# A hybrid decoder step: the samples' recurrence on VectorE, another closing order, and weight remainders by accumulating transfers

## The chip, the cores and the metric

The kernel runs on one core of one Trainium2 chip. Its five engines each have an instruction stream of their own: TensorE (PE) for matmuls and transposes, VectorE (DVE), ScalarE (ACT), GpSimd (POOL) and SyncE (SP). In this kernel SP issues nearly all transfers between DRAM and the on-chip memory (SBUF), and POOL issues a few. Matmul results land in a second on-chip memory (PSUM), which vector and scalar instructions read. The metric is the device time of one execution in microseconds (us).

## What is computed

The reference is one inference step of a two-layer decoder with width 1024, for a prompt of 1024 tokens and for 8 samples of one token each, which share all weights. Everything is float32. In outline, for the prompt and for the samples alike:

```
h = x
# layer 0
hn  = rmsnorm(h, g[0])
q, f, i, gate, q_m = split(hn @ w_in_a, 5)          # 512 columns each, 4 heads of 128
F = lb + (1 - lb) * sigmoid(f);  k = 1 - F;  v = i;  q = silu(q)
for each token: S = F[:, None] * S + k[:, None] * v[None, :];  o = q @ S     # per head, S is 128x128
mix = concat(rmsnorm(o) * silu(gate), attention(q_m, mem_k[0], mem_v[0])) @ w_o[0]
h = h + rmsnorm(mix);  h = h + rmsnorm(swiglu(rmsnorm(h)))
sb_k, sb_v = split(rmsnorm(h) @ w_kv)
# layer 1: stick-breaking attention over sb_k, sb_v (samples: over a paged cache), and memory attention
h = h + rmsnorm(concat(stick_breaking, attention(q_m, mem_k[1], mem_v[1])) @ w_o[1])
h = h + rmsnorm(swiglu(rmsnorm(h)))
swiglu(h) = (silu(h @ w_gate) * (h @ w_up)) @ w_down     # 2816 hidden columns: 22 blocks of 128
```

The samples start from given states `state_hgrn` (8 samples x 4 heads x 128 x 128) and take one step of the recurrence; the new states are an output (`st_sample`). Outputs also are `y_prompt`, `y_sample`, the shared keys and values, and the memory keys and values.

## The kernel before

**Split numbers.** TensorE multiplies in a format of fewer bits (float32r). So each operand is split into a rounded part and a remainder, and a product is made of three matmuls: high x high, high x low, low x high. For weights this is `split_w` (L196): a transfer of up to 4 blocks of 128x128 into `raw` (pool `wraw`, 5 buffers), a cast on ScalarE into `ws[:, 0]` (L206), and a subtraction on VectorE into `ws[:, 1]` (L207). The tiles `ws` come from the pool `wspl` with 5 buffers. `proj` (L212) calls it for the 4 or 8 blocks of a product and then issues the matmuls (L220). For activations it is `split_to` (L226).

**Tokens.** The prompt is worked in two halves: g = 0 has 512 columns, and g = 1 has the other 512 plus the 8 samples, 520 in all, done as two matmuls of 260. Activations stand with features on the partitions.

**Stages.** The program is a list of generators that `weave` merges by weights, step by step, so that the instruction streams hold pieces of several stages side by side. The framework's scheduler then orders each engine's instructions by priority and its own estimate of times, assigns buffers and sets the waits. Each engine works its own list in order. The stages that the change touches are:

- `hgrn_prompt` (L1147), the prompt's recurrence in 7 levels of doubling blocks, m = 1 to 64. At each level 16 calls per pair of heads and halves (L1174) make the products of a later block's queries with an earlier block's keys, 128 x m per chunk, and `copy_predicated` (L1184) puts them by a mask in the attention matrix `atts`.
- `hgrn_sample` (L1088), the samples' single step, woven with the gates and with part 1 of layer 0's feed-forward of g = 0. It turns k and v (L1096, L1097) so that samples stand on partitions, spreads v over a block diagonal (L1113), and makes k times v on TensorE (L1122). VectorE multiplies the state with F (L1117) and adds the product (L1123). For q times state, q is spread over a selection (L1105) and 32 small products go to TensorE (L1125). States come and go by SP (L1110, L1128).
- `ffn` (L697), the feed-forward of one half in five parts of 5, 5, 4, 4, 4 hidden blocks (`PARTS`). Each block has a gate and an up product over 8 blocks, and each part ends with 8 down products over its hidden blocks (L727). In layer 1 it serves g = 0 alone, beside the attention of g = 1 and of the samples, whose cache pages POOL fetches by index (L977).
- `weight_sums` (L549), sums of gate and up weights that POOL makes by accumulating transfers from DRAM to DRAM (L566; plain copies L568), each behind a tiny copy (L563) as a mark. They serve a multiplication scheme with fewer products (`ffn_w`, `gate_up_w`, L511), among other places in the last stage, layer 1's feed-forward of g = 1.
- `close` (L664), the last down products of that stage, with TensorE holding tokens on the moving side. It runs once for columns 0 to 255 (a = 0) and once for columns 256 to 519 with the samples (a = 1); weights are split in the first pass and kept for the second. After each pass `out_rows.finish` (L762) turns the result to rows, scales, adds the residual (L782, L785) and stores (L790; the samples L792).

## Time and profile before

| what | value |
|---|---|
| median of 3 runs (lowest, highest) | 2471.2 us (2469.78, 2472.68) |
| the profiled execution | 2472.22 us |
| its span, first to last instruction | 2470.5 us |
| granted clock of TensorE, mean | 0.999 |
| busy: TensorE, VectorE, ScalarE, POOL | 99%, 66%, 50%, 7% of the span |
| moved by transfers | 395.29 MB |

The profile's page gives busy times, a map of the span in 40 slices, the chain of work that ended last, groups of instructions, and transfers. A row of a group has the line, engine and operation, the tiles written and read, the count, then busy us and mean ns of one, then the idle time of the engine just before them and who ended it. A row of the chain has its start, its length in us and the work. TensorE's records overlap in the pipeline, so what a matmul costs is read from the distance of starts, or from the chain, and not from its own duration.

### The profile page before, as it was taken

Reading aid. Unit: us, or ns where it says so; the run is one execution under the profiler, and the core shown is the slowest. Engines: PE = TensorE matmul, PEld = TensorE weight load, DVE = VectorE, ACT = ScalarE, POOL = GpSimd, SP = SyncE. Lnnn points to the kernel's source line nnn. Section 1 sums busy time; section 2 is a strip of 40 time slices with the busy share of each in tenths; the row PEclk is TensorE's granted clock in tenths of the full one; section 3 lists DMA queues with packets and bytes.
Section 4 is the critical chain, followed back from the end, with each engine's and each line's share of the span. In section 5 each row is a group of like instructions: output and inputs, shape, how many; then the busy total and the mean of one; then the engine's idle time right before and its main releaser. Section 6 shows DMA issues by size and latency. Waiting matters only on the chain.

```text
span 2470.5 us, 42287 instructions
## 1 busy us (share of the span) xinstructions
PE 2436.5 (99%) x15971; PEld 2176.6 (88%) x15971; DVE 1639.5 (66%) x2988; ACT 1236.6 (50%) x2377; POOL 184.2 (7%) x316
## 2 busy tenths in 40 slices
PE   8999999999999999999999999999999999999998
PEld 6888888877879998899999989877777888999998
DVE  5767556754788685655756685778688466755666
ACT  5437544243445554555444554555554445664445
POOL 1000101100000000111200101212000100000000
PEclk9999999999999999999999999999999999999999
DMA  6354666546745437767666649754253573465542
GB/s 188 116 167 111 156 192 160 127 134 164 212 150 154 140 120 227 201 163 183 162 196 174 193 128 274 228 150 146 91 177 117 138 199 120 139 187 145 152 143 74
DMA packets 530503, 395.29 MB, mean 160 GB/s; under 512 B 21237, under 2 KB 468802, under 8 KB 530298
## 3 DMA queue, kind: packets, MB, share of 16 engines
q1 hardware_dynamic: 501114, 312.88, 42.4%
q0 software_dynamic: 29184, 79.70, 14.0%
q8 instruction: 126, 2.06, 0.3%
q14 instruction: 79, 0.65, 0.1%
HBM read 362.69 MB, written 101.11 MB: 188 GB/s over the span
## 4 chain that ended last, share of the span: by engine, by line
PE 88%; DVE 5%; DMA 3%; issue 2%; ACT 2%; POOL 0%; SPq 0%; DVEq 0%; ACTq 0%; POOLq 0%
PE mm L220 47%; PE q L511 13%; PE q L648 9%; PE q L464 3%; PE s L1174 2%; PE mm L1042 2%; PE s L906 1%; DMA c<-in_cache_mem_v 1%; PE s L1370 1%; PE mm L824 1%; PE mm L851 1%; PE q L680 1%; PE s L875 1%; PE s L1336 1%; PE s L899 1%
## 5 line engine op out<-in xcount | busy, mean ns | idle before, releaser
L220 PE MATMUL mm<-x,ws 128*128 128x260 f32 (+1 forms) x6240 | 1119.5, 335 | 3.2 <-DVE r L657 1.7
L220 PEld LDWEIGHTS mm<-x,ws 128*128 128x128 f32 x6240 | 941.6, 188 | 127.3 <-issue 2.7
L206 ACT CAST ws<-w 128x512 fp32r<-128x512 f32 (+1 forms) x652 | 382.8, 588 | 548.9 <-PE mm L220 396.9
L207 DVE TENSOR_TENSOR ws<-w,ws 128x512 fp32r<-128x512 f32 (+1 forms) x652 | 419.2, 648 | 253.5 <-ACT ws L206 243.5
L220 PE MATMUL mm<-m,ws 128*128 128x512 f32 (+1 forms) x1344 | 280.3, 360 | 0.5 <-DVE r L400 0.5
L220 PEld LDWEIGHTS mm<-m,ws 128*128 128x128 f32 x1344 | 218.0, 188 | 37.2 <-issue 1.0
L648 PE MATMUL q<-m,ws 128*128 128x260 f32 (+1 forms) x1824 | 221.7, 282 | 0.0
L648 PEld LDWEIGHTS q<-m,ws 128*128 128x128 f32 x1824 | 218.9, 188 | 1.1 <-DVE t L534 0.3
L502 DVE TENSOR_TENSOR ws<-w,ws 128x512 fp32r<-128x512 f32 x181 | 123.9, 690 | 87.6 <-ACT ws L501 86.1
L501 ACT CAST ws<-w 128x512 fp32r<-128x512 f32 x181 | 111.8, 621 | 109.2 <-PE q L648 32.5
L511 PE MATMUL q<-x,ws 128*128 128x260 f32 (+1 forms) x1188 | 158.1, 282 | 0.0
L511 PEld LDWEIGHTS q<-x,ws 128*128 128x128 f32 x1188 | 148.6, 188 | 0.0
L511 PE MATMUL q<-y,ws 128*128 128x260 f32 x912 | 119.9, 283 | 0.4 <-ACT q L521 0.2
L511 PEld LDWEIGHTS q<-y,ws 128*128 128x128 f32 x912 | 113.7, 189 | 1.1 <-ACT q L518 0.6
L464 PE MATMUL q<-x,ws 128*128 128x260 f32 (+1 forms) x720 | 91.3, 284 | 0.3 <-DVE r L400 0.2
L464 PEld LDWEIGHTS q<-x,ws 128*128 128x128 f32 x720 | 88.4, 188 | 1.8 <-DVE r L400 0.5
L511 PE MATMUL q<-a,ws 128*128 128x260 f32 (+1 forms) x672 | 87.1, 282 | 0.0
L511 PEld LDWEIGHTS q<-a,ws 128*128 128x128 f32 x672 | 83.2, 188 | 0.0
L657 DVE TENSOR_TENSOR r<-r,q 128x260 f32<-128x260 f32 (+1 forms) x128 | 48.4, 420 | 48.8 <-PE q L648 48.8
L237 DVE TENSOR_SCALAR t<-mm 128x512 f32<-128x512 f32 (+1 forms) x58 | 40.1, 691 | 54.1 <-PE mm L220 53.8
L563 POOL COPY mk<-a 128x1 f32<-128x1 f32 x36 | 21.0, 583 | 645.6 <-ACT a L1226 393.9
L228 DVE TENSOR_TENSOR m<-t,m 128x512 fp32r<-128x512 f32 (+1 forms) x88 | 60.8, 691 | 9.5 <-ACT m L227 8.7
(358 smaller groups left out, 3038.2 us busy)
## 6 DMA issues: line engine op xcount, KB each, us to landing
w<-in_w_gu SPq DMA_DIRECT2D x297, 256.0 KB, 3.4
w<-in_w_down SPq DMA_DIRECT2D x160, 256.0 KB, 2.8
wsum<-in_w_gu POOLq DMA_DIRECT2D x72, 512.0 KB, 6.5
w<-wsum SPq DMA_DIRECT2D x104, 256.0 KB, 3.5
w<-in_w_in_a SPq DMA_DIRECT2D x80, 256.0 KB, 3.3
w<-in_w_o SPq DMA_DIRECT2D x64, 256.0 KB, 2.8
wsum<-in_w_gu POOLq DMA_DIRECT2D x24, 640.0 KB, 7.0
wsum<-wsum POOLq DMA_DIRECT2D x24, 512.0 KB, 5.8
```

Source lines behind the costliest of these rows:

```text
L206: nc.scalar.copy(ws[:, 0, :n, :], raw[:, :n, :])
L207: nc.vector.tensor_sub(ws[:, 1, :n, :], raw[:, :n, :], ws[:, 0, :n, :].bitcast(F32))
L220: nc.tensor.matmul(ps[:, a, : PW[g]], wt, xt[k][:, xi, o : o + PW[g]], start=(k == 0 and wi == 0), stop=(k == nk - 1 and wi == 2),)
L228: nc.vector.tensor_sub(dst[1], src, dst[0].bitcast(F32))
L464: ins = nc.tensor.matmul(pp[a][:, :h], wt, xt[k][:, xi, a * h : (a + 1) * h], start=(k == 0 and wi == 0), stop=(k == ND - 1 and wi == 2),)
L501: nc.scalar.copy(w[:, 0, :], src)
L502: nc.vector.tensor_sub(w[:, 1, :], src, w[:, 0, :].bitcast(F32))
L511: nc.tensor.matmul(ps[:, :h], w[:, wj, k * P : (k + 1) * P], x[:, xi, :], start=(first and k == 0 and wi == 0), stop=(k == 3 and wi == 2), ...
L648: nc.tensor.matmul(pp[a][:, :h], wt, mids[k][:, xi, a * h : (a + 1) * h], start=(k == 0 and wi == 0), stop=(k == nf - 1 and wi == 2),)
L657: nc.vector.tensor_add(d, d, pp[a][:, :h])
L1042: nc.tensor.matmul(pb[i][:, a, :], xt[k][:, xi, c * P : (c + 1) * P], ws[:, s, :], start=(k == 0 and wi == 0), stop=(k == ND - 1 and wi == 2),
L1174: nc.tensor.matmul(plv[:, hh, c, :], K_[:, hh, cs], rhs, start=True, stop=True)
```

## The change

1. **The samples' recurrence.** k is no longer turned, and v is written to DRAM and read back broadcast over all partitions. VectorE multiplies the state with F, the broadcast v with k, adds them, and multiplies with q. TensorE then only sums over partitions: each half of a head's product is split and summed by two matmuls into one row of `po`, chosen by `selr`. The rows go through DRAM once more to be put in order. The constant `bdm` goes.
2. **The top level of `hgrn_prompt`** loads only the 64 key columns that are used, and puts the result by a plain copy on ScalarE.
3. **The closing order** becomes a = 1, then a = 0.
4. **Remainders by transfer.** In `ffn` of layer 1, g = 0, for the up and down weights: ScalarE writes the negated high part into the place of the remainder, and POOL issues a transfer that reads the weights from DRAM again and adds them there.

```diff
-    def split_w(W, k0, nk, m0, alloc=None):
+    def split_w(W, k0, nk, m0, alloc=None, acc=False):
...
             nc.scalar.copy(ws[:, 0, :n, :], raw[:, :n, :])
-            nc.vector.tensor_sub(ws[:, 1, :n, :], raw[:, :n, :], ws[:, 0, :n, :].bitcast(F32))
+            if acc:
+                nc.scalar.activation(ws[:, 1, :n, :], ws[:, 0, :n, :].bitcast(F32), AF.Copy, scale=-1.0)
+                nc.gpsimd.dma_start(ws[:, 1, :n, :], src, accum_op=ALU.add)
+            else:
+                nc.vector.tensor_sub(ws[:, 1, :n, :], raw[:, :n, :], ws[:, 0, :n, :].bitcast(F32))
...
-            for a in range(2):
+            for a in (1, 0):
...
-                    if a == 0:
+                    if a:
                         ws.append(split_w(w_down[l], f0, nf, m * P, self.spl4))
...
+            self.by_dma = g == 0 and l == 1
...
-                pu = proj(g, w_gu[l], 0, ND, DFF + (f0 + j) * P, self.xt)
+                pu = proj(g, w_gu[l], 0, ND, DFF + (f0 + j) * P, self.xt, self.by_dma)
...
-                ps = proj(g, w_down[l], f0, nf, m * P, mids)
+                ps = proj(g, w_down[l], f0, nf, m * P, mids, self.by_dma)
...
     def hgrn_sample(Ft, Kt, Qt, vs):
...
+        vd = tc.dram_tile([NB, 512], F32, name=nm("vd"))
+        nc.sync.dma_start(vd, vT[:NB, :])
+        yield
...
+            nc.sync.dma_start(vbv, vd[:, h * P : (h + 1) * P].partition_broadcast(P))
+            nc.vector.tensor_mul(stv, stv, col(Ft))
+            nc.vector.tensor_mul(vbv, vbv, col(Kt))
+            nc.vector.tensor_add(st, st, vb)
+            nc.sync.dma_start(st_sample[0, :, h].rearrange("b k v -> k b v"), stv)
+            nc.vector.tensor_mul(vbv, stv, col(Qt))
             for a in range(2):
-                ps = S()
-                nc.tensor.matmul(ps, kT[:NB, h * P : (h + 1) * P], vb[:NB, a, :], start=True, stop=True)
-                nc.vector.tensor_add(st[:, a, :], st[:, a, :], ps)
-            for b in range(NB):
-                nc.tensor.matmul(
-                    po[:NB, h * P : (h + 1) * P], qd[:, b, :], stv[:, b, :], start=(b == 0), stop=(b == NB - 1)
-                )
+                qs = B(F32R), B(F32R)
+                split_to(qs, vb[:, a, :])
+                for i, p in enumerate(qs):
+                    nc.tensor.matmul(
+                        po[:NB, :], selr[:, 2 * h + a, :], p,
+                        start=(h == 0 and a == 0 and i == 0), stop=(h == H - 1 and a == 1 and i == 1),
+                    )
+        rows = B()
+        nc.vector.tensor_copy(rows[:NB, :], po[:NB, :])
+        od = tc.dram_tile([H, NB, P], F32, name=nm("od"))
+        nc.sync.dma_start(od.rearrange("h (a b) v -> (h a) b v", a=2), rows[:NB, :].rearrange("p (b v) -> p b v", v=P))
         ot = B()
-        nc.vector.tensor_copy(ot[:NB, :], po[:NB, :])
+        nc.sync.dma_start(ot[:NB, :].rearrange("p (h v) -> p h v", v=P), od.rearrange("h b v -> b h v"))
...
+                        k = m if nbg == CH else P
+                        nc.tensor.matmul(
+                            plv[:k, hh, c, :], K_[:, hh, c * P : c * P + k], rhs, start=True, stop=True
+                        )
...
+                    if nb == 1:
+                        nc.scalar.copy(
+                            atts[hp * 2 + hh].rearrange("p (c t m) -> p c t m", c=CH, t=2)[:m, :, 1, :],
+                            plv[:m, hh, :, :],
+                        )
+                        continue
```

More of the change, by code (lines that the diff above doesn't have):

```diff
@@ L1088, in hgrn_sample, with col @@
     def hgrn_sample(Ft, Kt, Qt, vs):
-        HB = H * NB
-        kc = small([P, HB], tag="ss")
-        for h in range(H):
-            nc.vector.tensor_copy(kc[:, h * NB : (h + 1) * NB], Kt[h // 2][:, h % 2, G : G + NB])
-        pk = S()
         pvv = S()
         for h in range(H):
-            nc.tensor.transpose(pk[:NB, h * P : (h + 1) * P], kc[:, h * NB : (h + 1) * NB], ident)
             nc.tensor.transpose(pvv[:NB, h * P : (h + 1) * P], vs[:, h, :], ident)
-        kT = B()
-        nc.vector.tensor_copy(kT[:NB, :512], pk[:NB, :])
         vT = B()
         nc.vector.tensor_copy(vT[:NB, :512], pvv[:NB, :])
+        vd = tc.dram_tile([NB, 512], F32, name=nm("vd"))
+        nc.sync.dma_start(vd, vT[:NB, :])
+        yield
+        HB = H * NB
+        assert 2 * H == NB
         po = S()
         for h in range(H):
-            qd = small([P, NB, NB], tag="qd", bufs=2)
-            nc.vector.tensor_mul(
-                qd, sel, Qt[h // 2][:, h % 2, G : G + NB].unsqueeze(2).to_broadcast([P, NB, NB])
-            )
+            def col(t):
+                return t[h // 2][:, h % 2, G : G + NB].unsqueeze(2).to_broadcast([P, NB, P])
             st = C()
@@ L1173, in hgrn_prompt @@
                         rhs = Q_[:, hh, cs].rearrange("p (b t m) -> p b t m", t=2, m=m)[:, :, 1, :]
-                        nc.tensor.matmul(plv[:, hh, c, :], K_[:, hh, cs], rhs, start=True, stop=True)
+                        k = m if nbg == CH else P
+                        nc.tensor.matmul(
+                            plv[:k, hh, c, :], K_[:, hh, c * P : c * P + k], rhs, start=True, stop=True
+                        )
                 for hh in range(2):
@@ L1517, in tile_decoder @@
         nc.gpsimd.tensor_tensor(pidx, pidx, iot, op=ALU.add)
-        bdm = const.tile([NB, NB, 1], F32, name="bdm")
-        nc.gpsimd.affine_select(
-            bdm.rearrange("p b o -> p (b o)"), ones[:NB, :NB], pattern=[[-1, NB]], compare_op=ALU.is_equal,
-            fill=0.0, base=0, channel_multiplier=1,
-        )
     drain(head)
```

18 lines of the change are left out of this document (4 added, 14 removed).

## The prediction

> **What bounds the kernel now.** I read the page first (busy shares, chain by engine), then the chain of work and the waits of TensorE in the stages that the change touches, then single groups.
>
> ```profile
> span 2470.5 us, 42287 instructions
> PE 2436.5 (99%) x15971; PEld 2176.6 (88%) x15971; DVE 1639.5 (66%) x2988; ACT 1236.6 (50%) x2377; POOL 184.2 (7%) x316
> PE 88%; DVE 5%; DMA 3%; issue 2%; ACT 2%; POOL 0%; SPq 0%; DVEq 0%; ACTq 0%; POOLq 0%
> 520.00:616.00 96.00, 95.98 (x482) 73.22 (x481) 52.70 (x81) 36.26 (x61) 5.66 (x10) 0.98 0.56 152
> 1560.00:1955.00 395.00, 387.93 (x1887) 303.98 (x1886) 299.29 (x468) 207.46 (x399) 31.71 (x31) 1.00 0.47 140
> 1990.00:2092.00 102.00, 101.96 (x488) 83.94 (x487) 69.26 (x111) 52.35 (x85) 1.46 (x2) 1.00 0.52 152
> ```
>
> TensorE is busy all the time, and 88% of the chain is its work. The three window rows (length, then busy PE, weight loads, DVE, ACT, POOL; granted clock, DMA share) are the samples' recurrence, and the first half of layer 1's feed-forward in its two pieces. VectorE is at 76% in the second (299.29 of 395.00), and still TensorE is at 98%. So matmuls taken away are worth their own time; relief of VectorE is worth only what TensorE waits for it.
>
> **The samples' recurrence.** The chain from 520 to 620 us, by line, is in per cent of 100 us, so in us:
>
> ```profile
> by line: PE mm L220 80.2%; PE s L1125 8.4%; PE s L1122 7.6%; PE s L1213 0.9%; PE s L1209 0.9%; PE s L256 0.8%; PE s L1096 0.4%; PE s L1097 0.4%; PE s L1134 0.3%; PE s L1201 0.1%; issue 0.0%
> 1893.00 0.51 PE ns L948 x2
> 1918.04 0.46 PE ns L948 x2
> ```
>
> Gone are L1122 (k times v), L1125 (q times state) and L1096 (turning k): 7.6 + 8.4 + 0.4 = 16.4 us of TensorE. Added are 4 heads x 2 halves x 2 parts = 16 matmuls of the form of L948 (8 columns of `selr`, 512 moving): at 0.46/2 = 0.23 us, 3.7 us. Net 12.7 us less.
>
> ```profile
> L1117 DVE TENSOR_TENSOR c<-c,a x4: 1206/1214/1226, 354.5 to 561.7; 128x1024 f32<-128x1024 f32 x4
> L1113 DVE TENSOR_TENSOR c<-b,bdm x4: 1205/1210/1215, 528.8 to 564.1; 8x1024 f32<-8x1024 f32 x4
> L1105 DVE TENSOR_TENSOR qd<-sel,a x4: 224/224/226, 272.1 to 559.6; 128x64 f32<-128x64 f32 x4
> L1123 DVE TENSOR_TENSOR c<-c,s 128x512 f32<-128x512 f32 x8 | 5.4, 680 | 0.2 <-PE s L1122 0.2
> c<-in_state_hgrn SPq DMA_DIRECT2D x4, 512.0 KB, 5.4
> out_st_sample<-c SPq DMA_DIRECT2D x4, 512.0 KB, 4.9
> SPq L201 <- DVE ws L207: 1174.9, 506, 13.2
> ```
>
> VectorE per head: before 1.21 + 1.21 + 0.22 + 2 x 0.68 = 4.0 us; after 4 x 1.21 + 2 x 0.68 (split) = 6.2 us; four heads 9 us more, in a stage with 43 us idle: covered; without that cover it costs those 9 us. ScalarE gets 8 casts (5 us), also covered. SP gets 7 more transfers: v out to DRAM, four broadcasts of 512 KB back (5.4 us each by the state loads), and the rows out and back at the end. They stand in SP's queue ahead of weight loads, and a broadcast waits for the v write. SP is far ahead of need: 506 of its weight loads waited for a buffer that VectorE was still reading. I cost them at nothing; unhidden, each of the two round trips would cost about 10 us (5.4 + 4.9), bound 0 to 20. POOL loses one small select.
>
> **The top level of the prompt's scan (m = 64).** Its matmuls load 64 columns of K instead of 128, and eight predicated copies on VectorE become copies on ScalarE.
>
> ```profile
> 89.17 1.73 PE s L1174 x16
> L1174 PEld LDWEIGHTS s<-a,a x448: 186/192/193, 88.9 to 489.1; 128*128 128x128 f32 x150
> L1125 PEld LDWEIGHTS s<-c,qd x64: 85/90/133, 532.6 to 606.7; 128*8 128x8 f32 x64
> L1184 DVE COPY_PREDICATED b<-mask,s 128x256 f32<-128x256 uint8 x56 | 25.8, 525 | 0.0
> ```
>
> A record takes 1.73/16 = 0.108 us, though only 64 columns move, so I take the weight load to set its pace. A load of 128 columns takes 192 ns, of 8 columns 90: by a line between them, 64 columns take 138. The level has 448/7 = 64 records; 64 x 0.054 = 3.5 us is the upper end, 0 the lower; I take 2.0, since the next matmul can hide part. VectorE loses 8 x 0.525 = 4.2 us on which nothing waits, and ScalarE, idle half of the span, gains eight copies.
>
> The Trainium skill (TensorE: Matmul & The Clock Gate, LDWEIGHTS) says that a weight load's time is proportional to its columns alone, which would halve 0.108 and give 3.5 us. The trace disagrees at the small end, where 8 columns take 90 of 192 ns and not a sixteenth.
>
> **The closing order.** The chain's end, start and us:
>
> ```profile
> 2462.26 0.45 ACT yT L758
> 2465.87 0.65 DVE yT L782
> 2466.52 0.66 DVE yT L785
> 2467.21 0.30 SPq L792 DMA_DIRECT2D out_y_sample<-yT  x1
> DMA to landing us min/median/max: 2.6/2.6/2.6
> ```
>
> These rows are the sample's rows, which go to the middle, under the other half's matmuls. They free 0.45 + 0.65 + 0.66 = 1.8 us. But then the last store is a 512 KB row block, issued at about 2465.4 (2465.87 less 0.45) and landing 2.6 us later (the last row, that of the store of `y_prompt`), instead of the small one. I take 1.4 of the 1.8; lower end 0.5.
>
> **The remainders by DMA.** In layer 1's first half 22 x 2 up tiles and 56 down tiles (40 of 128x512, 16 of 128x128) are concerned: 100 subtractions leave VectorE, 100 negated copies go to ScalarE, and 100 accumulating transfers go to POOL's queue.
>
> ```profile
> L207 DVE TENSOR_TENSOR ws<-w,ws 128x512 fp32r<-128x512 f32 x588 | 401.4, 687 | 216.7 <-ACT ws L206 206.9 <-DMA w<-in_w_down 5.7 <-PE s L447 1.2
> L207 DVE TENSOR_TENSOR ws<-w,ws 128x128 fp32r<-128x128 f32 x64 | 18.3, 286 | 36.7 <-ACT ws L206 36.6
> L239 ACT ACTIVATE t<-t x42: 631/633/640, 399.4 to 1951.7; 128x512 f32<-128x512 f32 x32, 128x520 f32<-128x520 f32 x10
> L206 ACT CAST ws<-w 128x512 fp32r<-128x512 f32 x588 | 364.0, 620 | 473.6 <-PE mm L220 347.9 <-PE q L648 32.5 <-issue 24.7
> 1933.14 11.08 PE mm L220 x48
> wsum<-in_w_gu POOLq DMA_DIRECT2D x72, 512.0 KB, 6.5
> L566 POOL DMA_DIRECT2D wsum<-in_w_gu x64: 863/892/1297, 234.9 to 2000.0; - x64
> w<-in_w_gu SPq DMA_DIRECT2D x297, 256.0 KB, 3.4
> PE s L1370 <- ACT b L1367: 2.5, 2, 2.0
> 2000.02 0.87 POOL L566 DMA_DIRECT2D wsum<-in_w_gu  x1 [5.82 <-DMA wsum<-wsum]
> 2001.60 3.42 PE L220 MATMUL mm<-m,ws 128*128 128x512 f32 x14
> 1601.13 1.05 POOL L977 DMA_INDIRECT c<-in_cache_sb_k,pidx  x1 [26.04 <-DVE sc L934]
> PE s L1336 <- DVE b L1351: 1.1, 2, 0.8
> ```
>
> VectorE loses 84 x 0.687 + 16 x 0.286 = 62 us; ScalarE gains about 84 x 0.633 + 16 x 0.3 = 58 us, rising from 53% to about two thirds. The gain is bounded by TensorE's waits for vector work there; the rows of L1370 and L1336 are the longest of either kind, 3.6 us together. I take 2.0 less, bounds 0 and 4.
>
> The cost hangs on when a remainder is ready. A cast starts when TensorE frees one of five tiles (the release in L206's row). Four tiles lie ahead, 48 matmuls: 11.1 us, more where attention lies between. Down tiles of parts of five blocks have fewer, two tiles for 15 matmuls, so about 30: 7 us, but these parts are woven with attention. Against it stand the cast, 0.62, the negated copy, 0.63, and issue to landing. The nearest rows are a plain load of the same tile, 3.4, and a transfer of twice the size to DRAM, 6.5 (L566's accumulations hold POOL 0.89). Taking 4.5, nearer the plain load because bytes and shape are the same, the remainder is ready 5.8 us after the tile is free, at worst by these rows 7.8. So most of it is covered.
>
> Two places in POOL's queue are not. The sums for the last stage are still being made there; their last issue is at 2000.02, and the first down product of part 3 starts at 2001.60. An accumulation behind it lands at 2000.9 + 4.5 = 2005.4, its first use is two matmuls after 2001.60, at 2002.1: 3.3 us late, 5.3 by the 6.5; I take 4, bounds 0 and 6. And page loads of the cache hold POOL until VectorE frees a buffer (26.04 us once); accumulations behind one wait with it, and page loads now stand behind accumulations. Each was released by work of the same program place, so I take 2 for all of this, bounds 0 and 20.
>
> **The sum**, against the profiled execution's 2472.2 us: -12.7 - 2.0 - 1.4 - 2.0 + 4 + 2 = -12.1, so 2460.1. The median of the runs, 2471.2, is 1.0 lower: 2459.
>
> **Rivals.**
> *The remainders come too late (slower).* If a remainder needs N us from the freed tile, a turn of five tiles takes N plus a tile's own 2.8 us, or 13.9 when nothing waits. It decides from N = 11.1. With 100 tiles in some 20 turns, each us above costs about 20; N = 12.3 costs 24 and gives 2459 + 24 = 2483. For it: POOL's queue is in order, and ScalarE stands in the path twice. Against it: my estimate of 5.8, and 7.8 with the slower row.
>
> The Trainium skill (SBUF — State Buffer, A bandwidth-pool intuition that's wrong) bears on this rival. It says that descriptors of POOL's transfers cannot be written while VectorE runs a copy with both ports, and gives 3.1 us instead of 0.62. By that N would be some 2.5 us longer, 8.3, still under 11.1. The trace shows at most 1.30 against a usual 0.89 on L566.
>
> *The recurrence's matmuls go, but their time does not.* The new vector chain per head hangs on two loads, and at the end on two DRAM round trips. If TensorE stands in order before the 16 sums, 3 us per head eat 12 us: 2471, the same. Against it: 43 us of idle VectorE there.
>
> *All is hidden.* No collision at 2000 us, no late tile, both upper gains: -12.7 - 3.5 - 1.8 - 4 = -22, so 2449.
>
> **Chances.** Forecast 0.52, all hidden 0.17, recurrence without gain 0.13, too late 0.18. A difference under 0.2% (5 us) is no change to this measurement. Faster 0.69, same 0.13, slower 0.18. Range: from 2447, a little under all hidden, to 2483, the late case as priced; the forecast's own is 2452 to 2466.
>
> **What would show it.** Right: the chain from 520 to 620 has no L1122 or L1125, and 16 short products at 0.23 us; the sample's rows end before the last products; the new transfers land in 4 to 5 us; waits of TensorE for tiles whose remainder comes by DMA total under 10 us, most of it at the first down product of part 3. Wrong: landing over 9 us, or waits spread over all parts; or new waits of TensorE for the recurrence.

## The result, and the profile after

| | median (lowest, highest), us | ratio to before, 95% interval |
|---|---|---|
| before, beside it on the same chip | 2471.94 (2469.78, 2473.18) | |
| the changed kernel | 2492.85 (2488.54, 2496.17) | 1.0085 [1.0067, 1.0102] |

The change made the kernel 21 us slower. The prediction was 2459 us, and its range ended at 2483. The profiled execution took 2488.54 us; it is the lowest of its four runs, and 16.3 us above the profiled execution of before. The readings below explain these 16.3 us of the 21; the other runs have no profile.

The page of the changed kernel, by busy time, queues, chain, and groups:

```profile
span 2486.8 us, 42315 instructions
PE 2429.1 (98%) x15903; PEld 2174.4 (87%) x15903; DVE 1589.9 (64%) x2879; ACT 1291.2 (52%) x2493; POOL 311.3 (13%) x415
q1 hardware_dynamic: 505346, 315.02, 42.7%
q0 software_dynamic: 75840, 102.78, 21.5%
PE 83%; DMA 6%; DVE 5%; ACT 2%; issue 2%; POOL 0%; SPq 0%; DVEq 0%; ACTq 0%; POOLq 0%
L207 POOL DMA_DIRECT2D ws<-in_w_gu x44 | 57.9, 1352 | 180.1 <-ACT ws L206 146.9
L207 POOL DMA_DIRECT2D ws<-in_w_down x56 | 67.6, 1264 | 90.8 <-ACT ws L206 61.1
ws<-in_w_gu POOLq DMA_DIRECT2D x44, 256.0 KB, 6.0
ws<-in_w_down POOLq DMA_DIRECT2D x40, 256.0 KB, 5.7
```

TensorE has 7 us less to do than before (2429.1 against 2436.5), and VectorE 50. Still the span grew: TensorE's share of the chain fell from 88% to 83%, and that of DMA rose from 3% to 6%. The last two rows give the landing of the new transfers, 6.0 and 5.7 us at the median.

A queue's row has its packets, its MB, and the time that its packets took as a share of the time of 16 DMA engines. The row of GpSimd's queue in before:

```profile
q0 software_dynamic: 29184, 79.70, 14.0%
```

So 46,656 packets were added, of 495 bytes on average, and they took 21.5% of 16 x 2486.8 us less 14.0% of 16 x 2470.5 us: 65 ns each. A packet of SP's queue (q1), of 623 bytes on average, took 34 ns.

Where the time went is best seen by a ledger. The weight tiles are used in the same order in all kernels, but for 4 of 13,716 products in three of them. For each the table takes the start of its first matmul, less that of the same tile in before (negative is ahead of before). It is worked out from the matmul records of the two traces.

| place (time in before) | changed | lost or gained since the row above |
|---|---|---|
| 632, end of the samples' recurrence | -17.5 | -17.5 |
| 1476 | -16.8 | +0.7 |
| 1581, start of layer 1's first half of feed-forward | -15.0 | +1.8 |
| 1680 | -13.0 | +2.0 |
| 1768 | -6.4 | +6.6 |
| 1933 | -1.0 | +5.4 |
| 2002, before the first down product of part 3 | -1.0 | 0 |
| 2025, after these products | +11.8 | +12.8 |
| 2093, the down products of part 4 | +16.0 | +4.2 |
| 2440 | +16.4 | +0.4 |

At 632 us the first two parts of the change have given 17.5 us. The remainders take more than all of it back, in three places. (The 1.8 us lost ahead of 1581 are about what a stretch of 3.4 us at half clock costs, which this trace has at 1478.1 and before has not.)

The table compares single executions. How far they scatter can be seen from the four kernels that have the same transfers up to 1933 and the same order of TensorE's instructions from 1581 to 1933 (the changed kernel and, below, `e2_acc_only`, `e5_not_first_downs` and `e7_no_last_sums`): they lose 14.0, 17.0, 13.1 and 17.1 us there. A difference of 4 us between two ledgers beside the attention says little. Stages of the changed kernel in windows (length, busy PE, weight loads, DVE, ACT, POOL, then granted clock, DMA share, GB/s), which answer to the three window rows of before:

```profile
500.00:600.00 100.00, 99.96 (x542) 83.62 (x541) 68.16 (x103) 51.34 (x90) 7.96 (x11) 1.00 0.71 189
1566.00:1955.00 389.00, 373.06 (x1727) 287.79 (x1726) 249.34 (x373) 230.74 (x454) 117.45 (x98) 0.99 0.79 172
1990.00:2092.00 102.00, 89.52 (x417) 72.77 (x416) 41.93 (x67) 56.70 (x94) 29.10 (x24) 0.93 0.89 185
```

In the second row VectorE fell from 76% to 64% of the window, and TensorE's idle time rose from 7.1 us in 395 to 15.9 in 389. The DMA share went from 0.47 to 0.79. In the third row TensorE idles for 12.5 us in 102, where before has 0.04.

**The recurrence.** The chain from 500 to 604 us by line (per cent of 104 us), and the short products by form:

```profile
by line: PE mm L222 84.0%; PE s L1122 3.5%; PE s L1211 3.0%; PE s L258 2.9%; PE s L1223 2.6%; PE s L1219 2.6%; PE s L1205 1.3%; PE s L1094 0.4%; issue 0.0%
L1122 PE MATMUL s<-b,selr 128*8 128x512 f32 x16 | 4.3, 393 | 0.0
```

Products of k with v and of q with the state are gone. The 16 new ones take 3.5% of 104 us, 3.6 us, and nothing waits.

**The remainders.** TensorE's waits from 1566 to 2110 us (total, times, longest):

```profile
PE mm L222 <- DMA ws<-in_w_down: 13.4, 4, 10.5
PE s L1380 <- ACT b L1377: 7.4, 6, 2.4
PE s L1346 <- DVE b L1361: 4.3, 1, 4.3
```

The second and third are the rows L1370 and L1336 of before (2.5 and 1.1 us). The first row lies wholly at the down products of parts 3 and 4 (10.5 and 2.9 us). GpSimd's and then TensorE's timeline at the first of them:

```profile
2000.26 0.86 POOL L568 DMA_DIRECT2D wsum<-in_w_gu  x1 [6.08 <-DMA wsum<-wsum]
2001.02 4.05 POOL L207 DMA_DIRECT2D ws<-in_w_down  x3
...
2000.63 0.63 PE L222 MATMUL mm<-m,ws 128*128 128x512 f32 x2
2011.72 5.49 PE L222 MATMUL mm<-m,ws 128*128 128x512 f32 x12 [10.46 <-DMA ws<-in_w_down]
```

The window around them, and the transfers issued from 1998 to 2012 us (the last number is the median of us to landing):

```profile
1998.00:2018.00 20.00, 9.54 (x42) 7.76 (x41) 2.00 (x3) 5.25 (x9) 7.37 (x6) 0.66 1.13 234
```

```profile
ws<-in_w_down POOLq DMA_DIRECT2D x4, 256.0 KB, 11.0
```

The last sum for the next stage is issued at 2000.26, after 6.08 us in which GpSimd waited for another sum to land. Three accumulations follow at once. TensorE did two products with the first tile's high part and then waited 10.46 us. The window row shows why the transfers were slow: the DMA engines had more than they could do (share 1.13), and the four transfers issued there took 11.0 us at the median. It also shows a granted clock of 0.66: TensorE had half its clock for 13.7 us from 2003.8 on (0.34 x 20 / 0.5). Its 5.7 us of work in that time took twice what it should, 2.9 us more. 10.5 and 2.9 make 13.4, of which the ledger keeps 12.8.

How a late load delays TensorE though TensorE is not waiting for it is seen in five rows around 1795 us, from the timelines of VectorE, ScalarE and TensorE:

```profile
1791.66 1.23 DVE L936 TENSOR_TENSOR c<-c,b 128x1024 f32<-128x1024 f32 x1 [0.93 <-DMA b<-qd]
1792.92 1.22 DVE L937 TENSOR_REDUCE sc<-c 128x8 f32<-128x1024 f32 x1
...
1794.65 0.75 DVE L1361 TENSOR_SCALAR b<-s,biasp 128x512 f32<-128x512 f32 x1
...
1795.43 0.63 ACT L1332 ACTIVATE b<-b 128x512 f32<-128x512 f32 x1 [3.00 <-DVE b L1361]
...
1796.59 1.16 PE L1380 MATMUL s<-b,a 128*128 128x128 f32 x8 [1.17 <-ACT b L1377]
```

VectorE stands at the samples' scores (L936) until a broadcast of q lands. The prompt's L1361 is behind it in VectorE's order; ScalarE's L1332 waits 3.00 us for L1361, and L1377 is behind L1332; TensorE waits 1.17 us for L1377. Three queues in order pass the delay on. Of the 3.00 us only 0.93 are VectorE's wait for the load; the rest is the work that stands ahead of L1361.

### The profile page after: what moved, and what is told of

Read it like the earlier page. It is cut to its first block, busy times and chain, and to the rows that moved or that the text cites. A ratio compares the mean times of both kernels' runs of the same rounds, so it can differ in the third digit from the quotient of the medians.

```text
span 2486.8 us, 42315 instructions
## 1 busy us (share of the span) xinstructions
PE 2429.1 (98%) x15903; PEld 2174.4 (87%) x15903; DVE 1589.9 (64%) x2879; ACT 1291.2 (52%) x2493; POOL 311.3 (13%) x415
## 3 DMA queue, kind: packets, MB, share of 16 engines
q0 software_dynamic: 75840, 102.78, 21.5%
## 4 chain that ended last, share of the span: by engine, by line
PE 83%; DMA 6%; DVE 5%; ACT 2%; issue 2%; POOL 0%; SPq 0%; DVEq 0%; ACTq 0%; POOLq 0%
PE mm L222 43%; PE q L513 13%; PE q L650 9%; PE q L466 3%; PE s L1176 2%; PE mm L1045 2%; DMA b<-qd 1%; PE s L909 1%; PE s L1380 1%; PE mm L827 1%; PE mm L854 1%; PE q L682 1%; PE s L878 1%; DMA ws<-in_w_down 1%; PE s L1346 1%
## 5 line engine op out<-in xcount | busy, mean ns | idle before, releaser
L209 DVE TENSOR_TENSOR ws<-w,ws 128x512 fp32r<-128x512 f32 (+1 forms) x552 | 357.7, 653 | 227.0 <-ACT ws L204 217.7
L222 PE MATMUL mm<-m,ws 128*128 128x512 f32 (+1 forms) x1344 | 282.9, 363 | 13.5 <-DMA ws<-in_w_down 13.4
L207 POOL DMA_DIRECT2D ws<-in_w_gu x44 | 57.9, 1352 | 180.1 <-ACT ws L206 146.9
L207 POOL DMA_DIRECT2D ws<-in_w_down x56 | 67.6, 1264 | 90.8 <-ACT ws L206 61.1
```

The costliest lines, as they stand in the source:

```text
L207: nc.gpsimd.dma_start(ws[:, 1, :n, :], src, accum_op=ALU.add)
L209: nc.vector.tensor_sub(ws[:, 1, :n, :], raw[:, :n, :], ws[:, 0, :n, :].bitcast(F32))
L222: nc.tensor.matmul(ps[:, a, : PW[g]], wt, xt[k][:, xi, o : o + PW[g]], start=(k == 0 and wi == 0), stop=(k == nk - 1 and wi == 2),)
```

## The experiments

Each ratio is to runs of the kernel before on the same chip. "Ledger" is the table's measure, at 632, 1476, 1581, 1680, 1768, 1933, 2002, 2025, 2093 and 2440 us of before.

### The parts one by one

**All but the remainders** (`e1_no_acc`):

```diff
-            self.by_dma = g == 0 and l == 1
+            self.by_dma = False
```

> The changed kernel with all remainders made on VectorE again, so that only the recurrence, the top level and the closing order are left of the change. Theory: all of the loss comes with the accumulating transfers, and the rest gains what the starts of the feed-forward tiles show at 1566 us (15 to 17 us ahead of before): 2455 us, ratio 0.9935. Rival: the recurrence leaves a loss that only shows later (the 3 us given back near 1480 us are of it), then 2460 or more.

Measured: 2459.88 us, ratio 0.9941 [0.992, 0.9962]. Ledger -17.3, -15.6, -12.7, -12.4, and then -12.2 to -12.6 to the end. So the other three parts make the kernel faster, by a little less than they gain at first. The interval holds both forecasts; by the ledger nothing is given back behind 1581.

**The remainders alone** (`e2_acc_only`): the diff's `split_w`, `proj`, `by_dma` and the two calls in `ffn`, in the kernel before.

```diff
-            nc.vector.tensor_sub(ws[:, 1, :n, :], raw[:, :n, :], ws[:, 0, :n, :].bitcast(F32))
+            if acc:
+                nc.scalar.activation(ws[:, 1, :n, :], ws[:, 0, :n, :].bitcast(F32), AF.Copy, scale=-1.0)
+                nc.gpsimd.dma_start(ws[:, 1, :n, :], src, accum_op=ALU.add)
```

> The kernel before with the accumulating transfers alone. Theory: the loss of the changed kernel from 1566 us on, about 31 us, adds to the time of before: 2503 us, ratio 1.013. Rival: the loss comes from the two parts together, since the earlier stage shifts what meets in POOL's queue; then under 2490.

Measured: 2506.57, ratio 1.0132 [1.0106, 1.0158]. Ledger +1.6, +1.5, +2.4, +4.9, +11.4, +19.4, +19.4, +30.4, +33.9, +33.6. So the remainders cost 31 us by themselves from 1581 on, in the same places, as the theory had it.

**The recurrence alone** (`s1_sample_only`): the new `hgrn_sample`, and `bdm` gone.

```diff
+            nc.sync.dma_start(vbv, vd[:, h * P : (h + 1) * P].partition_broadcast(P))
+            nc.vector.tensor_mul(stv, stv, col(Ft))
+            nc.vector.tensor_mul(vbv, vbv, col(Kt))
+            nc.vector.tensor_add(st, st, vb)
```

> Only the samples' recurrence on VectorE is taken over; the top level, the closing order and the remainders are as before. The theory (TensorE's share goes nearly whole, the new vector chain and round trips are hidden) expects 15 us less than before, about 2457. The rival (part of the stage's gain belonged to the top level, or to a half-clock dip that does not return) expects 9 to 12 us less, 2460 to 2463.

Measured: 2458.51, ratio 0.994 [0.9919, 0.996]; ledger -15.9 at 632, -16.6 at the end. It gives all of the gain that the medians can show. The interval does not decide between 15 us and 9 to 12; the ledger speaks for the first, and some 1.7 us of it are a half-clock stretch that does not return.

**The top level alone** (`s2_level_only`):

```diff
+                        k = m if nbg == CH else P
+                            plv[:k, hh, c, :], K_[:, hh, c * P : c * P + k], rhs, start=True, stop=True
```

> Only the top level of the prompt's scan loads 64 columns. The 2.4 us seen at this place in the changed kernel's trace should come back as 2 us less at the end, about 2470; the upper end by the load alone is 3.5 us less, 2468.5. If the next matmul hides it, or it is given back later, 2472.

Measured: 2472.56, ratio 0.9996 [0.9985, 1.0006]. Ledger -2.7 at 632 and 1476, then +2.5 at 1581. The median cannot tell 2 us from nothing (2.6 us to either side). In the profiled execution the gain is there and is given back in one place. A wait of TensorE and a window of this kernel show it:

```profile
PE s L1345 <- DMA a<-ksc: 4.0, 1, 4.0
```

```profile
1566.00:1590.00 24.00, 20.01 (x127) 17.57 (x126) 13.22 (x23) 9.08 (x16) 4.09 (x4) 0.93 0.82 240
```

The first attention product of layer 1 waits for keys that come back from DRAM. This wait was 0.6 us in before, 4.0 here, and the clock falls behind it (0.93 over 24 us is 3.4 us at half). In `e1_no_acc` it was 2.4 us, and there the ledger fell by 2.9 between 1476 and 1581. In the recurrence alone it was 0.3, and nothing was lost. Why the keys come later in some of these kernels than in others was not settled.

**The closing order alone** (`s3_close_only`):

```diff
-            for a in range(2):
+            for a in (1, 0):
-                    if a == 0:
+                    if a:
```

> Only the closing order is changed. The tail behind the last product should be 1.3 us shorter, as in the changed kernel; the theory expects the two closing passes to be longer by as much, so no change, 2472. The prediction's rival is a gain of 1.4 us, 2470.5.

Measured: 2472.46, ratio 1.0002 [0.9991, 1.0013]. No gain is seen, though the interval (2.7 us to either side) could hide one of 1.4. In this run's trace the time from the last product to the end fell from 10.5 to 9.7 us (9.3 in the changed kernel), while the two passes of `close` took 27.5 us of TensorE's time instead of 26.2 (27.5 in the changed kernel): the turning of the samples' rows, which in before stood behind the last product, now lies between products.

### What the remainders cost, and why

**Transfers for parts 0 to 2 only** (`e3_acc_parts_0_2`):

```diff
-                pu = proj(g, w_gu[l], 0, ND, DFF + (f0 + j) * P, self.xt, self.by_dma)
+                pu = proj(g, w_gu[l], 0, ND, DFF + (f0 + j) * P, self.xt, self.by_dma and pi < 3)
-                ps = proj(g, w_down[l], f0, nf, m * P, mids, self.by_dma)
+                ps = proj(g, w_down[l], f0, nf, m * P, mids, self.by_dma and pi < 3)
```

> The changed kernel with accumulating transfers in parts 0 to 2 alone; parts 3 and 4 have their remainders from VectorE. Theory: the wait at the first down product of part 3, the half clock behind it and the late tiles of part 4 go, which the starts of tiles put at 12.8 + 4.2 = 17 us: 2476 us. Rival (the loss is spread evenly over the 100 tiles): 36 of the 100 are left out, so some 11 of 31 us go, 2482.

Measured: 2473.22, ratio 1.0006 [0.9991, 1.0021]. Ledger -17.8 at 1581, -16.3, -9.5, -3.3, and -3.3 from there on. Beside the attention 14.5 us are lost; without transfers in parts 3 and 4 nothing is lost after, as the theory had it.

**No transfers for part 3's down tiles** (`e5_not_first_downs`):

```diff
-                ps = proj(g, w_down[l], f0, nf, m * P, mids, self.by_dma)
+                ps = proj(g, w_down[l], f0, nf, m * P, mids, self.by_dma and pi != 3)
```

> The changed kernel, but part 3's eight down tiles have their remainders from VectorE. Theory: the wait of 10.5 us at the first of them and the half clock behind it (5.7 us of matmuls at half speed, 2.9 us) go: 2493 - 13 = 2480. Rival: POOL's queue is full there anyway and the wait moves to the first up tile of part 4: 2490.

Measured: 2479.41, ratio 1.0021 [1.001, 1.0032]. Ledger -1.3 at 1933, 2002 and 2025, then +2.6 at 2093. The 12.8 us are gone, as the theory had it; the loss at part 4 is not.

**Without part 4's sums** (`e7_no_last_sums`). The sums of part 4 are not made; part 3's are used in their place, so the last stage's part 4 works with other weights.

```diff
-    ws = weight_sums(1, range(5))
+    ws = weight_sums(1, range(4))
...
+    sums[1][4] = sums[1][3]
```

> The changed kernel without the 16 transfers that make part 4's sums; the last stage reads part 3's sums in their place, so its result for part 4 is another, with the same work. If the wait at the first down product of part 3 comes from the sums ahead of it in POOL's queue, it goes, as in the run without accumulation there: 2480. If it comes from the other loads that fill the transfer engines until 2004 us, some 5 us of it stay: 2486.

Measured: 2476.94, ratio 1.0013 [1.0001, 1.0025]. Ledger +2.1, +2.1, +1.8 at 1933, 2002 and 2025, +5.9 at 2093. All of part 3's down tiles still come by transfer, and nothing is lost at them: it was the sums ahead of them in GpSimd's queue and on the DMA engines. Part 4's loss has its own row here (TensorE's waits from 1995 us):

```profile
PE mm L222 <- DMA ws<-in_w_down: 2.9, 3, 1.4
```

Three short waits, 2.9 us, straight for remainders, with no sum near. The changed kernel has the same three, 0.73 us at 2086.95, 1.13 at 2091.11 and 1.12 at 2100.80. Its transfers issued from 2070 to 2097 us, and its window from 2077 to 2101:

```profile
ws<-in_w_down POOLq DMA_DIRECT2D x8, 256.0 KB, 9.1
2077.00:2101.00 24.00, 20.86 (x87) 15.59 (x86) 10.93 (x17) 13.95 (x24) 8.94 (x7) 1.00 1.27 253
```

These eight are part 4's down tiles. They landed after 7.6 to 11.9 us, 9.1 at the median, and each wait ends within 0.1 us of a landing. The DMA share there is 1.27, against 0.24 in the same window of before. The time that GpSimd needs to issue is not what made them late: each issue took 1.3 to 1.7 us, and ahead of seven of the eight GpSimd idled for 0.6 to 4.1 us. Each of these seven began 0.3 to 0.4 us after the transfer three places ahead had landed (the last four at 2087.21, 2091.38, 2094.00 and 2096.68, after landings at 2086.90, 2091.07, 2093.69 and 2096.38). So no more than three were under way there, and a late landing made a later issue late as well; what sets the limit is not shown.

**The negated copies without a transfer** (`e4_neg_no_dma`): ScalarE negates, VectorE adds the loaded tile.

```diff
-                nc.gpsimd.dma_start(ws[:, 1, :n, :], src, accum_op=ALU.add)
+                nc.vector.tensor_add(ws[:, 1, :n, :], raw[:, :n, :], ws[:, 1, :n, :].bitcast(F32))
```

> The changed kernel with the negated copies on ScalarE kept, but with VectorE adding the weights instead of the transfer: ScalarE has the same extra 58 us, POOL and the transfers nothing. If the loss in parts 0 to 2 comes from transfers and POOL's queue: 2456 us, as without any of it. If it comes from ScalarE, which stands in front of the attention's exponentials and copies: 2456 + 14 = 2470.

Measured: 2465.94, ratio 0.9973 [0.9959, 0.9988]. Ledger -17.0 at 1581, -17.2, -8.2, and -8.2 to -8.6 from there on. So 9 us are lost without any transfer, all between 1680 and 1768, and the time lies between the two forecasts. TensorE's longest waits there, and a window:

```profile
PE s L1346 <- DVE b L1361: 5.0, 2, 4.7
PE s L1380 <- ACT b L1377: 3.6, 2, 3.2
1676.00:1710.00 34.00, 28.01 (x112) 20.90 (x113) 22.94 (x32) 15.66 (x29) 6.31 (x6) 0.85 0.45 132
```

The granted clock, 0.85, stands for 10.2 us at half clock (0.15 x 34 / 0.5); `e1_no_acc` has none there. That it is ScalarE's added time that costs the 9 us is not shown, for the edit changed more than that: the scheduler ordered the stage anew. Of TensorE's 1622 instructions from 1581 to 1933 some 70 stand at another place of the list than in before and in `e1_no_acc`, which have one and the same order, and so do some 35 of VectorE's 320 other than weight subtractions. In the changed kernel it is some 130 of TensorE's.

**The negated copies on VectorE** (`e9_neg_on_vector`):

```diff
-                nc.scalar.activation(ws[:, 1, :n, :], ws[:, 0, :n, :].bitcast(F32), AF.Copy, scale=-1.0)
+                nc.vector.tensor_scalar(ws[:, 1, :n, :], ws[:, 0, :n, :].bitcast(F32), -1.0, None, op0=ALU.mult)
```

> The changed kernel with the negated copy made by VectorE instead of ScalarE; the transfers stay. The kernel with copies on ScalarE but no transfer lost 9 us between 1680 and 1705 us against the one without either. Theory: those 9 us go and the loss by transfers stays: 2484. Rival: the place in the chain counts, not the engine; then the time is that of the changed kernel, 2493.

Measured: 2504.17, ratio 1.0121 [1.0095, 1.0147]. This was a miss on both sides: it is no better than the changed kernel, and worse by its median. Its ledger loses at all places: -12.2 at 1581, -6.4, +3.1, +12.8, +12.8, +30.9, +35.1. Between 1680 and 1768 it loses 9.5 us with no copy on ScalarE, so ScalarE's load cannot be the cause here (TensorE's order is another one again). It also waits longer for remainders, 19.2 us against 13.4. That the transfer now begins when VectorE, the busier engine, has come to the copy would explain this; it was not tried apart:

```profile
PE mm L222 <- DMA ws<-in_w_down: 19.2, 5, 9.1
```

**Up tiles only** (`e8_ups_only`):

```diff
-                ps = proj(g, w_down[l], f0, nf, m * P, mids, self.by_dma)
+                ps = proj(g, w_down[l], f0, nf, m * P, mids)
```

> The changed kernel with accumulating transfers for the 44 up tiles alone; the 56 down tiles go by VectorE. Theory: down tiles, which have the short cover and meet the sums at the first down products of part 3, are what comes late, and up tiles cost only their share of the copies on ScalarE, 44 of 100 times 9 us or 4 us: 2460 + 4 = 2464, and no wait of TensorE for a remainder. Rival: up tiles are late too, or what stands behind them in the queue of GpSimd is: 2469 or more.

Measured: 2465.29, ratio 0.9969 [0.9953, 0.9984]. Ledger -18.3 at 1581, -17.0, -12.6, -9.1, and -9.0 to -9.1 from there on; no wait for a remainder. The time is as the theory had it. Its reason does not fit as well: of the 7.9 us lost from 1680 to 1933, 3.5 lie behind 1768, where the copies alone cost nothing (a difference within the scatter named above).

### Copies, traffic, or waiting

Open was what is lost between 1768 and 1933: 5.4 us in the changed kernel, 6.2 with parts 0 to 2, nothing with the copies alone. Two runs were to show it by spare transfers that no product needs.

**A spare target** (`e6_spare_target`): VectorE makes all remainders, GpSimd reads the same 100 tiles into a spare place in DRAM.

```diff
-                nc.scalar.activation(ws[:, 1, :n, :], ws[:, 0, :n, :].bitcast(F32), AF.Copy, scale=-1.0)
-                nc.gpsimd.dma_start(ws[:, 1, :n, :], src, accum_op=ALU.add)
+                spare = tc.dram_tile([P, 4, P], F32, name=nm("spare"))
+                with tc.issue_after(cast.ins):
+                    nc.gpsimd.dma_start(spare[:, :n, :], src)
```

> The changed kernel with all remainders from VectorE, and POOL copying the same 100 weight tiles to a spare place in DRAM that nobody reads: the transfers' traffic and POOL's queue without anyone waiting for a remainder. If traffic and queue alone cost time (page loads later, other loads slower): 2465 or more. If only the waiting for remainders costs: 2460, as without accumulation.

**Copies and a spare target** (`e10_neg_and_spare`): the same, behind the negated copy, to which VectorE adds the loaded tile.

```diff
+                cast = nc.scalar.activation(ws[:, 1, :n, :], ws[:, 0, :n, :].bitcast(F32), AF.Copy, scale=-1.0)
                 with tc.issue_after(cast.ins):
                     nc.gpsimd.dma_start(spare[:, :n, :], src)
+                nc.vector.tensor_add(ws[:, 1, :n, :], raw[:, :n, :], ws[:, 1, :n, :].bitcast(F32))
```

> The changed kernel, but VectorE adds the loaded tile to the negated copy; GpSimd issues a transfer of the same 100 tiles after the same copies, into a spare place in DRAM that nobody reads. So ScalarE's copies and the traffic are there together, and no product waits for a transfer. Theory A (copies and traffic together delay the samples' attention): TensorE loses about 9 us at 1680 to 1705, and 4 to 6 us at 1790 to 1870, and nothing at the first down products of part 3: 2470. Theory B (what is lost at 1790 to 1870 is waiting for the remainders themselves): nothing lost there, 2465.

Measured: 2469.68, ratio 0.9983 [0.997, 0.9996], and 2476.94, ratio 1.0006 [0.9993, 1.0018]. Both lose nothing between 1768 and 1933 (-6.5 to -7.1, and +5.5 to +5.3), and that looked like an answer. It was none. The spare transfers of `e6_spare_target` by line (first and last start at the end):

```profile
L208 POOL DMA_DIRECT2D spare<-in_w_down x56: 534/714/1350, 19.1 to 106.3; - x56
L208 POOL DMA_DIRECT2D spare<-in_w_gu x44: 668/714/1503, 3.3 to 97.1; - x44
```

The edit's `issue_after` did not hold them back, and all 100 ran in the first 107 us. So in layer 1 these two kernels have no added traffic; they repeat `e1_no_acc` and `e4_neg_no_dma` there. The lost 10 and 14 us at the kernel's start, where these transfers ran, are what lifts their times (ledger at 632: -7.4 and -3.1 instead of -17 to -19).

**Traffic in its place** (`e12_traffic`, and with the negated copies `e11_neg_and_traffic`). Each spare transfer stands behind a one-column mark on GpSimd that needs the cast; it accumulates in one of 12 places in DRAM.

```diff
+                mark = nc.gpsimd.tensor_copy(small([P, 1], tag="mk", bufs=1), ws[:, 0, 0, 0:1].bitcast(F32))
+                with tc.issue_after(mark.ins):
+                    to = spare[len(turn) % 12][:, :n, :]
...
+                        nc.gpsimd.dma_start(to, src, accum_op=ALU.add)
+                turn.append(0)
+            nc.vector.tensor_sub(ws[:, 1, :n, :], raw[:, :n, :], ws[:, 0, :n, :].bitcast(F32))
```

> As the run before, without the negated copies: VectorE makes all remainders as in the kernel before, and the marked spare transfers run beside. Theory A: 4 to 6 us at 1790 to 1870, and little at 1680 to 1705: 2464. Theory B, or copies and traffic only together: 2460.

> ScalarE makes the negated copies, VectorE adds the loaded tile to them, and GpSimd issues accumulating transfers of the same 100 tiles to 12 spare places in DRAM that nobody reads, each behind a one-column mark that waits for ScalarE's cast (the first 12 are plain copies). Unlike the earlier spare transfers, which all ran in the first 107 us, these must run in layer 1's first half. Theory A (the traffic delays the loads of q and of the cache, and with them the attention): TensorE loses 4 to 6 us at 1790 to 1870 beside the copies' 7 to 9 us at 1680 to 1705, nothing at the first down products of part 3: 2471. Theory B (waiting for the remainders): nothing at 1790 to 1870, 2465.

Measured: 2482.04, ratio 1.0035 [1.0023, 1.0046] with traffic alone; 2491.12, ratio 1.0073 [1.0056, 1.009] with copies and traffic. Ledger of the first: -16.2 at 1581, -11.6, -6.7, +8.7 at 1933, 2002 and 2025 (8.8), +11.7 at 2093. Of the second: -12.7, -6.2, +2.8, +12.9, 13.0, 13.6, +16.0. No product of theirs waits for one of these transfers, and little or nothing is lost from 2002 to 2025 (the first's 2.9 us at 2093 are a wait of 2.55 us for VectorE); but beside the attention the traffic alone loses 25 us. The comparison is clean: from 1581 to 1933 TensorE's instructions stand in the order of `e1_no_acc`, which loses 0.4 us there, and in the second run in that of `e4_neg_no_dma`, which loses 8.6 where this one loses 25.6. Theory A stands as to the cause, and the loss is far more than expected. It is more than the changed kernel's own, too: these transfers go from DRAM to DRAM and not into SBUF, and the marks and transfers hold GpSimd 137 us in the window below (117 in the changed kernel). So these runs show the cause, not its size.

The sign of it is how long VectorE waits for q's broadcasts from 1560 to 1960 us. In order: before, the copies alone, the changed kernel, traffic alone (total, times, longest).

```profile
DVE c L933 <- DMA b<-qd: 1.8, 5, 0.8
```

```profile
DVE c L936 <- DMA b<-qd: 1.3, 4, 0.5
```

```profile
DVE c L936 <- DMA b<-qd: 15.0, 9, 3.3
```

```profile
DVE c L943 <- DMA b<-qd: 17.9, 10, 3.4
```

These broadcasts are issued by SP, so GpSimd's queue is not what holds them. Where VectorE waited for one, it came 3.9 to 5.6 us after its issue in before, 5.0 to 8.4 in the changed kernel and 4.1 to 7.8 with the traffic alone. Cache pages, which do stand in GpSimd's queue, are not the cause: VectorE's waits for pages of `cache_sb_v` are 4.1 us in before and 4.8 with the traffic alone (9.5 in the changed kernel, but 8.3 with the copies alone, which have no transfer). The same 389 us in windows, for `e1_no_acc`, `e4_neg_no_dma` and `e12_traffic`, beside the changed kernel's row above:

```profile
1566.00:1955.00 389.00, 383.06 (x1827) 297.98 (x1828) 289.33 (x452) 200.27 (x386) 32.18 (x41) 1.00 0.45 133
```

```profile
1566.00:1955.00 389.00, 378.57 (x1779) 293.92 (x1778) 287.61 (x446) 234.61 (x458) 34.48 (x34) 0.99 0.44 129
```

```profile
1566.00:1955.00 389.00, 365.69 (x1678) 281.48 (x1677) 281.20 (x436) 191.06 (x371) 136.59 (x172) 0.98 0.75 168
```

TensorE's busy time falls from 383 to 379 with the copies, and to 366 with the traffic (DMA share 0.45 to 0.75). VectorE's own load hardly differs.

## Why the prediction was wrong

By its own terms, against the profiled execution:

| term | predicted | measured | from |
|---|---|---|---|
| recurrence | -12.7 | -16.6 | ledger of `s1_sample_only` |
| top level | -2.0 | -2.4 at its place, 0 at the end | ledger, `s2_level_only` |
| closing order | -1.4 | 0, give or take 2.7 | `s3_close_only` |
| VectorE's relief in layer 1 | -2.0 (0 to -4) | none; with traffic, copies and the new order +14 | ledger 1581 to 1933 |
| the first down product of part 3 | +4 (0 to 6) | +12.8 | ledger, `e5_not_first_downs`, `e7_no_last_sums` |
| page loads and other late tiles | +2 (0 to 20) | +4.2, part 4's down tiles; no loss found by page loads | ledger, waits of VectorE |

The measured rows add up to +14.4 of the 16.3 us; most of the rest is the 1.8 us ahead of 1581.

**The recurrence** went as the prediction said: the lines are gone, the 16 products cost 3.6 us (3.7 predicted), and VectorE's longer chain and the trips through DRAM are hidden. It is 3.9 us better. About 1.7 of these are a half-clock stretch of 3.4 us that before had at 532.7 and that does not come back; for the rest no row was found. The rival "their time does not go" fell, and with the waits at 2001 us so did "all is hidden".

**The top level** was sized rightly, as far as one trace shows. The row of the loads has 132 ns at its least, where the line between 90 and 192 gave 138 (the range of the row is that of all levels):

```profile
L1176 PEld LDWEIGHTS s<-a,a x448: 132/192/193, 90.1 to 488.1; 128*128 128x128 f32 x128, 128*64 128x64 f32 x22
```

What failed is that the gain was carried to the end unasked. It was lost at the next wait whose other side is a transfer, with a half-clock stretch on top.

**The closing order** counted what leaves the tail and not that the same work lands among products that bound.

**The remainders** carry the error, in three steps of the prediction.

First, "the gain is bounded by TensorE's waits for vector work there" looked only at the side of VectorE that got lighter. This term was to be -2.0, and 14 us were lost. The waits rose, from 3.6 us to 11.7 for the rows of L1370 and L1336. Two things did it that the prediction had as harmless or did not have. The transfers' traffic delayed loads of other stages: this is shown (`e12_traffic`, in an unchanged order of instructions). And 100 copies more, together with the other order that the scheduler then chose, cost 9 us without any transfer (`e4_neg_no_dma`); which of the two it was is open. ScalarE was to rise "from 53% to about two thirds" and has 59% in the window. The prediction priced an added transfer by its own landing, and gave no price to what 100 more of them do to the landing of others. The two do not add up: with both the changed kernel loses 14 us there, the copies alone 9 and the traffic run alone 25.

Second, at the first down product of part 3 the place and the mechanism were right, and the size was not: "lands at 2000.9 + 4.5". The first one was issued at 2001.02, but the transfers there landed after 11.0 us, with the DMA share at 1.13. A landing set between medians of the whole span (3.4 and 6.5) was used at the one place of which the prediction itself said that transfers collide there. And a wait of 10.5 us costs TensorE its clock: 2.9 us more.

Third, for part 4's down tiles the cover of 11.1 us did not hold: 2.9 us of direct waits and 4.2 in the ledger. The landing was the wrong term again: 9.1 us at the median there, not 4.5. From the start of the negated copy to the landing these eight tiles took 8.6 to 13.9 us, seven of them over 11. That GpSimd needs 1.26 to 1.35 us to issue each, where the prediction had read 0.89 off another form, is not what made them late: GpSimd idled between the issues, each of which came only after the landing of the transfer three ahead.

The rival "too late" was right in sign, and its mechanism came true at one place alone. It had each turn of tiles stretched once N passes 11.1 us. Ahead of 1955 us copy and landing took 6.5 us at the median, and in parts 0 to 2 TensorE never waited for a remainder; at part 4's down tiles N did pass 11.1, and that cost 4.2 us and not 24. The order in which the losses appear also answers the prediction's own test: its bound of 10 us on these waits was passed (13.4), most of it at the place it named, and the landing passed 9 us at the two places that waited.

What stays open: how the 14 us in layer 1 divide between copies, order and traffic in the changed kernel itself, and why the keys' load is late in some kernels that only start it earlier.

## What to carry to other kernels

Work moved from a busy engine to idle ones is not free because these have room: ask whose chain the new instruction stands in, and which other loads the new traffic will delay. Price a transfer at the place where it is needed, by the transfers that are under way there, and not by a median; the queue ahead of it and the DMA share of that window are the rows to read. Where a scheduler places the instructions, a change in one engine's work can order the whole stage anew; compare the orders of two kernels before their difference is put down to the edit. A gain that reaches a later wait for a transfer has to be followed past that wait: the recurrence alone (ratio 0.994) beats both kernels, and nothing that was added to it made it measurably faster.

## What was not expected of the hardware

An accumulating transfer of 256 KB into SBUF landed after 5.7 to 6.0 us at the median, where a plain load of the same tile took 3.4; with the engines full it took 11.0 (share 1.13) and 9.1 (share 1.27). Its packets took 65 ns for 495 bytes, those of SP's queue 34 ns for 623. Issuing one held GpSimd for 1.26 to 1.35 us, against 0.89 for the sums.

Short waits of TensorE can cost its clock as well. The wait of 4.35 us at 1682.5 in the changed kernel, and that of 3.99 us at 1580.8 in `s2_level_only`, were each followed by 3.4 us at half clock, up to 1.7 us of work more. A wait of 2.42 us was enough in `e1_no_acc` (timeline of TensorE, and a window with its granted clock: 0.11 x 15 / 0.5 is 3.3 us at half):

```profile
1566.26 1.42 PE L1346 MATMUL s<-a,a 128*128 128x128 f32 x4 [2.42 <-DMA a<-ksc]
```

```profile
1560.00:1575.00 15.00, 12.58 (x66) 10.21 (x65) 5.54 (x10) 4.14 (x7) 0.00 (x0) 0.89 0.76 258
```

The Trainium skill (TensorE: Matmul & The Clock Gate, HAM oscillation) warns of idle gaps of more than about 3.4 us. The length at half clock agrees with its window; the gap does not, since here 2.42 us did it. Nor does the length of a wait decide alone: 2.55 us at 2098.8 in `e12_traffic` were followed by no such stretch, and before has one at 532.7 with no wait over 1.3 us in the 400 us ahead of it.
